# Token sums at another byte, attention from h's first result, and three smaller moves in a decoder layer on one core

## The chip, the cores and the metric

The kernel runs on 1 core of one Trainium2 chip. The metric is the device time of one execution in microseconds (us). All inputs and the output are float32.

## The reference

One decoder layer on 512 tokens of width 2048: a combined input projection, differential attention with 8 heads beside a gated short convolution, an output projection, and a SwiGLU feed-forward network of width 5632, each half between two RMS norms.

```python
hn = rms_norm(x, norm_mix_pre[l])
proj = hn @ w_in[l]                       # 2048 -> 6 x 1024
q, k, v, gate_b, gate_c, hc = jnp.split(proj, split_at, axis=-1)
...
a = diff_attention(q, k, v, lam, rel_bias)
a = rms_norm(a, subln_gain[l], SUBLN_EPS) * (1.0 - lambda_init)
a = a.reshape(b, s, A)
c = gate_b * short_conv(gate_c * hc, conv_w[l])
c = rms_norm(c, conv_norm_gain[l])
mix = jnp.concatenate([a, c], axis=-1) @ w_out[l]
x = x + rms_norm(mix, norm_mix_post[l])
hn = rms_norm(x, norm_ffn_pre[l])
f = (jax.nn.silu(hn @ w_gate[l]) * (hn @ w_up[l])) @ w_down[l]
x = x + rms_norm(f, norm_ffn_post[l])
```

In `diff_attention` a head has two softmaxes over 64 channels each, w = softmax(q1 k1 + bias) - lam * softmax(q2 k2 + bias), causal, and the output is w v.

## The kernel before

**Products.** Every float32 product of the large matrices is three matmuls (L133 to L135): both operands are split into a high part (a cast, on ACT, L99) and a low part (the rest, a subtraction on DVE, L100), and high x high, high x low and low x high are summed in PSUM. Weights come from HBM by DMA into raw tiles, are split into the four places of the ring `ring_all`, and feed PE from there. The normed tokens stay in one tile, `acts`, as `act_hi` and `act_lo`.

**Stages.** The start norms x and computes the first half of v (bank after bank pv, one for each of four blocks of 128 tokens, t). Then come jobs in a list; `run_jobs` runs them in order and gives a step of the side work (`side`) between their steps:

- the second half of v, with the token sums `t_sums` as side work;
- `project`: q, k and the first 256 columns each of h and c, as 10 quartets of 256 columns (8 for q and k, then h and c), each by 7 products instead of 8 (Strassen). A product is 24 matmuls of 128x256. Four of the seven (5, 7, 6, 4) read sums of token blocks, kept in `t_all` at the offset that `t_part` gives; three (1, 2, 3) read `acts`. In quartets 1 and 4 (`CLOSE_QK`) the products 1, 2, 5, 7 stand in this order, in the others 1, 5, 7, 2, and the instruction order lets four matmuls of one product through ahead of the one before;
- `open_attn` closes the pool `wino` (t_all, odd_raw, the r tiles) and opens `attn` in its place;
- column jobs (`job_cols`) of 256 columns: h1, b0, c1, b1, h2, c2, b2, h3, c3, b3, each with two halves of K and two banks pc, so 24 matmuls of 128x512 for each half and bank (a step), with the gated convolution in `done_h`, `done_c`, `done_b`. Attention is side work beside them: `heads` starts, in each step, the scores of one query block (pss, L658, then bias and exponential on DVE and ACT into e), the transposed weights of the block before (ptw, L688) and the values of the one before that (pa, L701); `head_out` (pta) ends a head. With 8 heads of 4 blocks that is some 37 steps. `load_attn`, a job after h1, issues the loads of q and k of head 0, of v and of the convolution's y, and puts `heads` on the side list. b0 and b1 are `finer`: they also give a side step in the middle of each 24 matmuls;
- output projection, residual, norms;
- `ffn`: gate and up in quartets by 7 products (banks pa, pb, pd), with token sums in tiles x and weight sums made by `combine(q, s)`: the sum s = 1 of the next quartet after product 3 of this one, in place in the order on DVE; only for q == HEAD it is held behind the low part of the split of product 3 (`issue_after`). `store_h` writes the hidden values out;
- down projection, and `down_last`, which adds the last products, norms a block of 128 tokens and stores it: per block t four pieces of 512 columns, each one DVE operation f * r + x (L1514) and a store, from SP's queue for even and from ACT's for odd pieces.

**What sets the order.** Each engine runs its own queue in order. PE's order is that of the program's steps, and PE waits for whichever operand is last. A new tile in a pool that opens where another was closed waits for the whole use of the old one.

**Places.** The operands' start in a partition, modulo 512 bytes, is fixed by the pools: `act_hi` and `act_lo` in `project` 480, the ring there 32; in `ffn` the tokens 416, the token sums in x 32, the ring 480. `t_all` starts at byte 20512 before, and its first sum 16 elements on, at 96 of 512.

Of the kernel before, what the change touches and what calls it, by code (L numbers as in the profile page):

```python
# [11 lines left out]
F32 = mybir.dt.float32  # L12
F32R = mybir.dt.float32r
AF = mybir.ActivationFunctionType
ALU = mybir.AluOpType
# [3 lines left out]
P = 128  # L19
D = 2048  # L20
S = 512
NT = S // P
KC = D // P
A = 1024
NH = 8
# [30 lines left out]
def trunk(ctx: ExitStack, tc: tile.TileContext, a, out):  # L56
    nc = tc.nc
    w_in, w_out, w_gate, w_up, w_down = (a[n][0] for n in ("w_in", "w_out", "w_gate", "w_up", "w_down"))
    x = a["x"][0]
    out = out[0]  # L60
# [102 lines left out]
    side = []  # L163
    done_ = object()

    def add_job(specs, go, ahead=1):
        jobs.append((specs, go, ahead))
# [142 lines left out]

    wino = ExitStack()
    wn = wino.enter_context(tc.tile_pool(name="wino", bufs=1))
    t_all = wn.tile([P, 8 * D + 16], F32R, name="t_all")
    odd_raw = [wn.tile([P, D], F32, name=f"odd{i}") for i in range(2)]


# [4 lines left out]
    for i in range(2):  # L321
        nc.vector.tensor_tensor_reduce(
            out=lamv[:, 2 * i, :], in0=lamv[:, 2 * i, :], in1=lamv[:, 2 * i + 1, :], scale=1.0, scalar=0.0,
            op0=ALU.mult, op1=ALU.add, accum_out=lamd[:, i : i + 1],
# [19 lines left out]

    def evacuate(cg, t, bank):

        if t % 2 == 0:
            tmp["v"] = wn.tile([P, 2, 512], F32, tag="r", bufs=2, name=f"r_v{cg}_{t}")
        nc.scalar.copy(tmp["v"][:, t % 2, :], bank)
        if t % 2:  # L350
            nc.sync.dma_start(vd[:, t - 1 : t + 1, cg * 512 : (cg + 1) * 512], tmp["v"])

    tmp = {}
    for t in range(NT):
        evacuate(0, t, vb[t])

# [3 lines left out]
    def open_attn(_):  # L360
        nonlocal ap_, aT, cT, v_sb, sqacc, klos
        wino.close()
        ap_ = at.enter_context(tc.tile_pool(name="attn", bufs=1))
        v_sb = ap_.tile([P, NT, A], F32, name="v_sb")
        aT = ap_.tile([P, NH, S], F32, name="aT")
        cT = ap_.tile([P, 8, S], F32, name="cT")
        sqacc = ap_.tile([P, S], F32, name="sqacc")

        klos = [ap_.tile([P, 2, S], F32R, name=f"klo{i}") for i in range(2)]
        for t in klos:  # L370
            nc.gpsimd.memset(t.bitcast(F32), 0.0)
        return
        yield

    def load_attn(_):
        load_qk(0)
        nc.sync.dma_start(v_sb, vd)
        nc.sync.dma_start(cT[:, 0:2, :], yd)
        side.append(heads(range(NH)))
        return  # L380
        yield

# [19 lines left out]
    def col_spec(w, c0, half, name):  # L402
        return w[half * 1024 : (half + 1) * 1024, c0 : c0 + 256], 8, 256, f"{name}_{half}"

    def job_cols(w, c0, name, done, finer=False):

        banks = []

        def part(half):
            def go(ch):  # L410
                (hi, lo), = ch
                for j in range(2):
                    if half == 0:
                        banks.append(mm_bank(f"pc_{name}_{j}"))
                    for k in range(8):
                        kc = 8 * half + k
                        cs = slice(j * P, (j + 1) * P)
                        mm3(banks[j], hi[:, k, cs], lo[:, k, cs], act_hi[:, :, kc, :], act_lo[:, :, kc, :], kc == 0, kc == KC - 1)
                        if finer and k == 3:
                            yield  # L420
                    if half == 1:
                        done(j, banks[j])
                    yield

            return go

        for half in range(2):
            add_job([col_spec(w, c0, half, name)], part(half))
# [15 lines left out]
    raws_qk, operands_qk = {}, {}  # L444

    def t_part(i, part):
        return t_all[:, 16 + (2 * T_PLACE[i] + part) * D :][:, :D].rearrange("p (t k n) -> p t k n", t=2, n=P)

    def t_sums():

# [272 lines left out]
    held = {}  # L723

    def done_h(j, b):
        t = ap_.tile([P, S + 2], F32, tag="hs", bufs=2, name=f"hs_{j}")
        nc.gpsimd.memset(t[:, 0:2], 0.0)
        nc.scalar.copy(t[:, 2:], b)
        held[j] = t
# [35 lines left out]
    for p in range(1, 4):  # L765
        job_cols(w_in, 5 * A + p * 256, f"h{p}", done_h)
        if p == 1:
            add_job([], load_attn)
            job_cols(w_in, 3 * A, "b0", done_b(0), finer=True)
        job_cols(w_in, 4 * A + p * 256, f"c{p}", done_c(p))  # L770
        job_cols(w_in, 3 * A + p * 256, f"b{p}", done_b(p), finer=p == 1)

    def as_tokens(t):
        return t.rearrange("p (t n) -> p t n", n=P)
# [624 lines left out]
    def ffn(_):  # L1399
        ready, ng = 7, len(order)  # L1400
        for n in (5, 6):
            prepare(n)
        for n, (q, i) in enumerate(order):
            product(n)
            yield
            gather(n)
            if n == 4:
                load_quartet(1)
            if q + 1 < HEAD and i in (6, 3):
                combine(q + 1, {6: 1, 3: 3}[i] if q else {3: 1, 6: 3}[i])  # L1410
            elif q < last_q and i == 3:

                with tc.issue_after(made[q, 3][1]) if q == HEAD else ExitStack():
                    combine(q + 1, 1)
            while ready < n + (5 if ready < ng and order[ready] in STAGED else 4):
                prepare(ready)
                ready += 1
            if i == 7 and q > 0:
                finish(q - 1)
            if i == 6 and q > 0:  # L1420
                store_h(q - 1)
            if q == last_q:

                for j, t in {1: ((1, 0),), 2: ((1, 1), (2, 0), (2, 1)), 5: ((5, 0),), 3: ((5, 1), (3, 0), (3, 1))}.get(
                    i, ((i, 0), (i, 1))
                ):
                    load_slot(j, 0, (t,))
        finish(last_q)
        store_h(last_q)
        load_block(1, 0)  # L1430
        for n, (g, cb, i, hf) in enumerate(steps):
            in_turn(steps_down, n, n + 2 if i == 3 and hf == 0 and 4 * g + cb in CLOSE_D else None, 7)
            yield
            gather_down(n)
            while ready < min(ng + n + 4, ng + len(steps)):
                prepare(ready)
                ready += 1
            if cb == 3 and hf == 1:
                load_slot(i, g + 1)
            if g == 2 and cb == 3:  # L1440
                tail_loads(i, hf)
# [37 lines left out]
    def down_last(_):  # L1479
        for t in range(NT):  # L1480
            xt = place(f"x{4 + t % 2}")
            nc.sync.dma_start(xt, x1d[t])

            pieces = [(cg, 0, 512) for cg in range(4)]
            if t == NT - 1:
                pieces[3:] = [(3, 0, 256), (3, 256, 256)]
            n = len(pieces)
            ssf = small.tile([P, n], F32, tag=f"ss{n}", name=f"ssf_{t}")
            for at_, (cg, c0, w_) in enumerate(pieces):
                cs, ws = slice(cg * 512 + c0, cg * 512 + c0 + w_), slice(c0, c0 + w_)  # L1490
                m = late["f"][:, t, cs]
                b = (mm_bank, aux_bank)[t % 2](f"pd_l_{cg}_{t}_{c0}")[:, :w_]
                for k in range(4):
                    ks = 4 * (k % 2) + t
                    mm3(
                        b, act_hi[:, k // 2, ks, :], act_lo[:, k // 2, ks, :], ch[cg][0][:, k, ws], ch[cg][1][:, k, ws],
                        k == 0, k == 3,
                    )
                nc.vector.tensor_add(m, m, b)
                nc.scalar.activation(b, m, AF.Square, accum_out=ssf[:, at_ : at_ + 1])  # L1500
                if at_ == n - 1:
                    ss = small.tile([P, 1], F32, tag="ss1", name=f"ssl_{t}")
                    v = small.tile([P, 1], F32, tag="v1", name=f"v_fin{t}")
                    nc.vector.reduce_sum(ss, ssf, axis=mybir.AxisListType.X)
                    mean = nc.vector.tensor_scalar(out=v, in0=ss, scalar1=1.0 / D, scalar2=EPS, op0=ALU.mult, op1=ALU.add)
                    r = small.tile([P, 1], F32, tag="r1", name=f"r_fin{t}")
                    nc.gpsimd.tensor_tensor(out=r, in0=v, in1=mhalf[:, :1], op=ALU.pow)
                with tc.issue_after(mean.ins) if (t, at_) == (NT - 1, n - 1) else ExitStack():
                    nc.vector.tensor_mul(m, m, late["gfin"][:, cs])
                if c0 + w_ == 512:  # L1510
                    yield
            for c in range(4):
                cs = slice(c * 512, (c + 1) * 512)
                nc.vector.scalar_tensor_tensor(  # L1514
                    out=xt[:, cs], in0=late["f"][:, t, cs], scalar=r, in1=xt[:, cs], op0=ALU.mult, op1=ALU.add
                )
                (nc.scalar if c % 2 else nc.sync).dma_start(out[t * P : (t + 1) * P, cs], xt[:, cs])

    add_job([], ffn, ahead=0)
# [29 lines left out]
```

## Time and profile before

| what | us |
|---|---|
| median of 3 runs | 2069.55 (2068.45 to 2071.57) |
| the profiled execution | 2067.07 |
| its span, first to last instruction | 2065.3 |
| start with the first half of v; second half of v | 0 to 113.2 |
| `project` | 113.2 to 311.4 |
| column jobs with attention | 311.4 to 594 |
| output projection, residual, start of `ffn` | 594 to 850 |
| gate and up | 850 to 1630 |
| down and the end | 1630 to 2065.3 |

A profile row of a group gives line, engine, operation, tiles (out<-in), shape and count, then the busy time in all, the mean of one in ns, and the idle time of the engine before, with what ended it. A matmul's duration is longer than the step from one start to the next, since matmuls are pipelined; the step is read from the start times in the timeline, or from the time of a stretch over its count. A row of the waits names the engine and operation that waited, and for what. A row of the windows gives the stretch, its length, PE's busy time with the number of matmuls, the granted clock, the DMA's busy share and GB/s.

### The profile page before, as it was taken

The page shows a single profiled execution, that of the slowest core. Times are in us where ns is not written, and L with a number is a line of the kernel's source. Part 1 is how long each engine was busy: PE and PEld are TensorE (multiplying, and loading weights), DVE is VectorE, ACT ScalarE, POOL GpSimd, SP SyncE. Part 2 cuts the span into 40 slices and gives each one's busy share as a digit, 9 for nine tenths or more (in the row PEclk, how much of TensorE's full clock was granted, in tenths as well). Part 3 has the DMA queues.
Part 4 walks back from the last instruction along what each step waited for, and adds up shares of the span by engine and source line. Part 5 has one row for each costly group of instructions (what it writes and reads, how often), then busy time and mean ns, then how long its engine had stood idle before and what let it go on. Part 6 is the DMA issues. An engine that isn't in the chain of part 4 may idle for free.

```text
span 2065.3 us, 36338 instructions
## 1 busy us (share of the span) xinstructions
PE 2044.6 (99%) x15356; PEld 1939.9 (94%) x15356; DVE 1626.4 (79%) x2058; ACT 969.3 (47%) x1361; POOL 27.4 (1%) x49
## 2 busy tenths in 40 slices
PE   9999999999999999999999999999999999999998
PEld 7899998888888889999999999999999999999996
DVE  5777767887465468989888988889889777888887
ACT  4444445664334354544544544544554444434442
POOL 0000001000000000000000000000000000000000
PEclk9999999999999999999999999999999999999999
DMA  7444326322239857654554653554654955748354
GB/s 244 131 160 143 124 93 211 100 92 87 82 107 363 299 208 288 194 159 131 181 159 125 187 159 125 187 159 124 188 159 132 331 179 198 266 126 301 112 190 163
DMA packets 301907, 359.64 MB, mean 174 GB/s; under 512 B 11912, under 2 KB 261768, under 8 KB 295856
## 3 DMA queue, kind: packets, MB, share of 16 engines
q1 hardware_dynamic: 300144, 351.53, 51.3%
q10 hardware_dynamic: 1600, 5.79, 0.9%
q8 instruction: 120, 1.97, 0.4%
q14 instruction: 43, 0.35, 0.1%
HBM read 289.64 MB, written 70.28 MB: 174 GB/s over the span
## 4 chain that ended last, share of the span: by engine, by line
PE 90%; DVE 4%; DMA 2%; issue 2%; ACT 1%; POOL 0%; SPq 0%; DVEq 0%; POOLq 0%; ACTq 0%
PE pb L134 7%; PE pb L133 7%; PE pb L135 7%; PE pd L135 6%; PE pd L134 6%; PE pd L133 6%; PE pa L133 5%; PE pa L134 5%; PE pa L135 5%; PE po L133 3%; PE po L134 3%; PE po L135 3%; PE pqk_b L133 2%; PE pqk_b L135 2%; PE pqk_b L134 2%
## 5 line engine op out<-in xcount | busy, mean ns | idle before, releaser
L99 ACT CAST ring_all<-raw_q 128x1024 fp32r<-128x1024 f32 x124 | 129.8, 1050 | 189.0 <-PE pb L134 72.3
L134 PE MATMUL pb<-x,ring_all 128*128 128x256 f32 x696 | 194.8, 280 | 0.0
L134 PE MATMUL pb<-acts,ring_all 128*128 128x256 f32 x704 | 194.5, 276 | 0.0
L133 PE MATMUL pb<-acts,ring_all 128*128 128x256 f32 x704 | 194.5, 276 | 0.0
L135 PE MATMUL pb<-acts,ring_all 128*128 128x256 f32 x704 | 194.4, 276 | 0.0
L133 PE MATMUL pb<-x,ring_all 128*128 128x256 f32 x696 | 194.2, 279 | 0.0
L135 PE MATMUL pb<-x,ring_all 128*128 128x256 f32 x696 | 194.2, 279 | 0.0
L133 PE MATMUL pa<-acts,ring_all 128*128 128x256 f32 x680 | 188.6, 277 | 0.0
L134 PE MATMUL pa<-acts,ring_all 128*128 128x256 f32 x680 | 188.1, 277 | 0.0
L135 PE MATMUL pa<-acts,ring_all 128*128 128x256 f32 x680 | 187.9, 276 | 0.0
L135 PE MATMUL pd<-ring_all,acts 128*128 128x256 f32 x640 | 176.8, 276 | 0.3 <-DMA acts<-hx 0.3
L133 PE MATMUL pd<-ring_all,acts 128*128 128x256 f32 x640 | 176.8, 276 | 0.0
L134 PE MATMUL pd<-ring_all,acts 128*128 128x256 f32 x640 | 176.7, 276 | 0.0
L99 ACT CAST ring_all<-pre 128x1024 fp32r<-128x1024 f32 (+1 forms) x106 | 105.1, 996 | 141.0 <-PE pb L134 73.7
L100 DVE TENSOR_TENSOR ring_all<-raw_q,ring_all 128x1024 fp32r<-128x1024 f32 x124 | 151.5, 1222 | 22.4 <-ACT ring_all L99 22.1
L100 DVE TENSOR_TENSOR ring_all<-pre,ring_all 128x1024 fp32r<-128x1024 f32 (+1 forms) x106 | 122.1, 1155 | 46.3 <-ACT ring_all L99 45.6
L99 ACT CAST ring_all<-post 128x1024 fp32r<-128x1024 f32 (+1 forms) x106 | 105.2, 994 | 95.7 <-PE pd L135 38.7
L100 DVE TENSOR_TENSOR ring_all<-post,ring_all 128x1024 fp32r<-128x1024 f32 (+1 forms) x106 | 121.9, 1150 | 15.1 <-ACT ring_all L99 15.1
L134 PE MATMUL pd<-ring_all,x 128*128 128x256 f32 x480 | 132.6, 276 | 0.3 <-DVE ring_all L100 0.3
L135 PE MATMUL pd<-ring_all,x 128*128 128x256 f32 x480 | 132.5, 276 | 0.0
L133 PE MATMUL pd<-ring_all,x 128*128 128x256 f32 x480 | 132.5, 276 | 0.0
L133 PEld LDWEIGHTS pb<-acts,ring_all 128*128 128x128 f32 x704 | 132.2, 188 | 0.0
(358 smaller groups left out, 6598.8 us busy)
## 6 DMA issues: line engine op xcount, KB each, us to landing
raw_q<-in_w_gate SPq DMA_DIRECT2D x42, 1024.0 KB, 5.4
post<-in_w_up SPq DMA_DIRECT2D x22, 1024.0 KB, 5.2
pre<-in_w_up SPq DMA_DIRECT2D x22, 1024.0 KB, 5.3
hx<-spare SPq DMA_DIRECT2D x20, 896.0 KB, 8.2
hx<-m SPq DMA_DIRECT2D x20, 896.0 KB, 8.9
raw_o<-in_w_out SPq DMA_DIRECT2D x16, 1024.0 KB, 8.0
raw_b<-in_w_down SPq DMA_DIRECT2D x16, 896.0 KB, 5.9
acts<-hx SPq DMA_DIRECT2D x32, 448.0 KB, 9.0
```

Source lines behind the costliest of these rows:

```text
L99: first = nc.scalar.copy(hi, src)
L100: second = nc.vector.tensor_tensor(out=lo, in0=src, in1=hi.bitcast(F32), op=ALU.subtract)
L133: yield nc.tensor.matmul(o, lhsT=lhi, rhs=rhi, start=start, stop=False, **kw).ins
L134: yield nc.tensor.matmul(o, lhsT=lhi, rhs=rlo, start=False, stop=False, **kw).ins
L135: yield nc.tensor.matmul(o, lhsT=llo, rhs=rhi, start=False, stop=stop, **kw).ins
```

## The change

Five things, in one diff:

1. The token sums start 112 elements into `t_all` instead of 16. With part 2 `t_all` begins at byte 28704, and the first sum at 480 of 512, the same as act_hi and act_lo in `project`.
2. The first tile for v's copies, r_v0_0, is allocated ahead of `t_all`, in the place where `t_all` began.
3. The loads of `load_attn` move into `open_attn`, ahead of h1, and `heads` is put on the side list by the first `done_h`, in the last steps of h1. `finer` is gone: every column job gives a side step after each 24 matmuls only.
4. The sum s = 1 for the quartet after HEAD - 1 is held behind the split of product 3 too.
5. In the last token block the piece c = 2 is scaled on ACT and added on GpSimd (POOL), where DVE did both in one operation.

```diff
+    tmp = {"v": wn.tile([P, 2, 512], F32, tag="r", bufs=2, name="r_v0_0")}
-    t_all = wn.tile([P, 8 * D + 16], F32R, name="t_all")
+    t_all = wn.tile([P, 8 * D + 112], F32R, name="t_all")
...
     def evacuate(cg, t, bank):
-        if t % 2 == 0:
+        if t % 2 == 0 and (cg, t) != (0, 0):
             tmp["v"] = wn.tile([P, 2, 512], F32, tag="r", bufs=2, name=f"r_v{cg}_{t}")
...
-    tmp = {}
...
             nc.gpsimd.memset(t.bitcast(F32), 0.0)
-        return
-        yield
-
-    def load_attn(_):
         load_qk(0)
         nc.sync.dma_start(v_sb, vd)
         nc.sync.dma_start(cT[:, 0:2, :], yd)
-        side.append(heads(range(NH)))
...
-    def job_cols(w, c0, name, done, finer=False):
+    def job_cols(w, c0, name, done):
...
-                        if finer and k == 3:
-                            yield
...
-        return t_all[:, 16 + (2 * T_PLACE[i] + part) * D :][:, :D].rearrange("p (t k n) -> p t k n", t=2, n=P)
+        return t_all[:, 112 + (2 * T_PLACE[i] + part) * D :][:, :D].rearrange("p (t k n) -> p t k n", t=2, n=P)
...
     def done_h(j, b):
+        if "begun" not in held:
+            held["begun"] = True
+            side.append(heads(range(NH)))
...
         if p == 1:
-            add_job([], load_attn)
-            job_cols(w_in, 3 * A, "b0", done_b(0), finer=True)
+            job_cols(w_in, 3 * A, "b0", done_b(0))
         job_cols(w_in, 4 * A + p * 256, f"c{p}", done_c(p))
-        job_cols(w_in, 3 * A + p * 256, f"b{p}", done_b(p), finer=p == 1)
+        job_cols(w_in, 3 * A + p * 256, f"b{p}", done_b(p))
...
-                with tc.issue_after(made[q, 3][1]) if q == HEAD else ExitStack():
+                with tc.issue_after(made[q, 3][1]) if q in (HEAD - 1, HEAD) else ExitStack():
                     combine(q + 1, 1)
...
-                nc.vector.scalar_tensor_tensor(
-                    out=xt[:, cs], in0=late["f"][:, t, cs], scalar=r, in1=xt[:, cs], op0=ALU.mult, op1=ALU.add
-                )
+                m = late["f"][:, t, cs]
+                if (t, c) == (NT - 1, 2):
+                    nc.scalar.activation(m, m, AF.Copy, scale=r)
+                    nc.gpsimd.tensor_tensor(out=xt[:, cs], in0=m, in1=xt[:, cs], op=ALU.add)
+                else:
+                    nc.vector.scalar_tensor_tensor(out=xt[:, cs], in0=m, scalar=r, in1=xt[:, cs], op0=ALU.mult, op1=ALU.add)
```

How the change moves instructions, at three places. First PE's queue where attention begins; pss are the first scores of head 0, q and k its operands, pc_b0_0 and pc_b0_1 the two banks of b0, pc_h1_1 the second of h1. Before:

```order
L135 MATMUL pc_b0_0_3024<-acts_72,ring_all_73 128x512
L658 MATMUL pss_0_0_0_3070<-k_0_3038,q_0_3037 128x128
L659 MATMUL pss_0_0_0_3070<-klo0_2905,q_0_3037 128x128
L658 MATMUL pss_0_0_1_3071<-k_0_3038,q_0_3037 128x128
L659 MATMUL pss_0_0_1_3071<-klo0_2905,q_0_3037 128x128
L133 MATMUL pc_b0_1_3089<-acts_72,ring_all_73 128x512
```

In this place of the changed kernel's queue, at the end of h1:

```order
L135 MATMUL pc_h1_1_2937<-acts_72,ring_all_73 128x512
L651 MATMUL pss_0_0_0_3041<-k_0_2994,q_0_2993 128x128
L652 MATMUL pss_0_0_0_3041<-klo0_2905,q_0_2993 128x128
L651 MATMUL pss_0_0_1_3042<-k_0_2994,q_0_2993 128x128
L652 MATMUL pss_0_0_1_3042<-klo0_2905,q_0_2993 128x128
L133 MATMUL pc_b0_0_3064<-acts_72,ring_all_73 128x512
```

The first scores moved ahead by the 24 matmuls of b0's first bank; the scores after them (pss_0_1) stand 24 matmuls on instead of 12, and the first transpose (ptw_0_0) 8 matmuls after those, in b0's second bank.

Second, DVE's queue in `ffn` where the first sum of quartet 4 is made (m1 from the two raw tiles raw_q4); post and pre are the weights of the quartet at work, and ring_all<-post and ring_all<-pre the low parts of their splits. Before:

```order
L100 TENSOR_TENSOR ring_all_73<-post_55_7158,ring_all_73 128x1024
L1068 TENSOR_TENSOR m1_52_6979<-raw_q4_0_7305,raw_q4_1_7306 128x1024
L1235 TENSOR_TENSOR m3_57_7309<-m3_57_7309,spare_58_7315 128x1792
L1072 TENSOR_TENSOR post_55_7158<-pre_56_7159,post_55_7158 128x8x128
L1197 TENSOR_TENSOR m0_53_7010<-pb_2_7248,m1_52_6979 128x512
L1074 TENSOR_TENSOR pre_56_7159<-pre_56_7159,post_55_7158 128x8x128
L100 TENSOR_TENSOR ring_all_73<-post_55_7158,ring_all_73 128x1024
L1070 TENSOR_TENSOR raw_q4_0_7305<-raw_q4_0_7305 128x8x128
L100 TENSOR_TENSOR ring_all_73<-pre_56_7159,ring_all_73 128x1024 x2
```

The same piece of the changed kernel:

```order
L100 TENSOR_TENSOR ring_all_73<-post_55_7158,ring_all_73 128x1024
L1068 TENSOR_TENSOR post_55_7158<-pre_56_7159,post_55_7158 128x8x128
L1231 TENSOR_TENSOR m3_57_7309<-m3_57_7309,spare_58_7315 128x1792
L100 TENSOR_TENSOR ring_all_73<-post_55_7158,ring_all_73 128x1024
L1193 TENSOR_TENSOR m0_53_7010<-pb_2_7248,m1_52_6979 128x512
L1070 TENSOR_TENSOR pre_56_7159<-pre_56_7159,post_55_7158 128x8x128
L100 TENSOR_TENSOR ring_all_73<-pre_56_7159,ring_all_73 128x1024 x2
L1064 TENSOR_TENSOR m1_52_6979<-raw_q4_0_7305,raw_q4_1_7306 128x1024
L1179 TENSOR_TENSOR m2_54_7011<-m2_54_7011 128x256
```

The sum (L1068 before, L1064 after) moved from the second row to behind the three splits, and raw_q4's next difference (L1070 before) further on still.

Third, ACT's queue at the end, where f holds the last block and pd_l its last banks. Before:

```order
L1500 ACTIVATE pd_l_3_0_20202,ssf_20185<-f 128x512
L1500 ACTIVATE pd_l_3_0_20218,ssf_20185<-f 128x512
L1500 ACTIVATE pd_l_3_0_20234,ssf_20185<-f 128x256
L1500 ACTIVATE pd_l_3_256_20250,ssf_20185<-f 128x256
L1517 DMA out<-x_192_20183 128x512 x2
```

And in the changed kernel:

```order
L1496 ACTIVATE pd_l_3_0_20218,ssf_20185<-f 128x512
L1496 ACTIVATE pd_l_3_0_20234,ssf_20185<-f 128x256
L1496 ACTIVATE pd_l_3_256_20250,ssf_20185<-f 128x256
L1513 ACTIVATE f<-f,r_fin_20269 128x512
L1517 DMA out<-x_192_20183 128x512 x2
```

ACT's scaling (L1513) is new ahead of its two stores; DVE's last row (f * r + x) counts three pieces instead of four, and POOL has one new row behind the last r_fin, the addition into x_192.

## The prediction

> **What bounds the kernel now.** I read the page's first part, then the busy time by stage, then the waits of PE, and only then single instructions.
>
> ```profile
> PE 2044.6 (99%) x15356; PEld 1939.9 (94%) x15356; DVE 1626.4 (79%) x2058; ACT 969.3 (47%) x1361; POOL 27.4 (1%) x49
> ```
>
> PE is busy for 2044.6 of 2065.3 us, so time can come off in two ways only: PE waits less, or its matmuls follow each other more closely. The PE windows of four stages show both (busy us, number of matmuls, granted clock):
>
> ```profile
> 113.20:311.40 198.20, 198.20 (x1681) 1.00 0.37 123
> 333.20:424.00 90.80, 87.61 (x454) 1.00 0.38 125
> 424.00:594.00 170.00, 169.81 (x843) 1.00 0.26 84
> 850.00:1630.00 780.00, 779.97 (x6754) 1.00 0.52 161
> ```
>
> At full clock and without a wait, `project` (113.2 to 311.4) takes 198.20/1681 = 117.9 ns from one matmul to the next, while gate/up (850 to 1630) takes 780.0/6754 = 115.5 ns, with the same tile of 128x256. Column jobs b0, c1 and b1 (333.2 to 424) leave PE idle for 90.80 - 87.61 = 3.2 us; the jobs after them leave 0.2 us. The waits of PE that the change touches, over the whole span (total, times, longest):
>
> ```profile
> PE pa L701 <- DVE wlo L100: 1.4, 2, 0.9
> ...
> PE pd L135 <- DVE ring_all L100: 1.2, 1, 1.2
> PE ptw L688 <- DVE e L677: 0.9, 2, 0.7
> PE pa L701 <- ACT aT L721: 0.9, 1, 0.9
> PE pv L133 <- ACT r_v L349: 0.7, 1, 0.7
> ```
>
> **Part 1, the token sums' place.** First the mean duration by form, in `project` (two rows), then in gate/up (three rows; each form has three such rows, L133 to L135):
>
> ```profile
> L133 PE MATMUL pqk_b<-t_all,ring_all 128*128 128x256 f32 x240 | 67.2, 280 | 0.0
> ...
> L133 PE MATMUL pqk_a<-acts,ring_all 128*128 128x256 f32 x160 | 45.0, 281 | 0.0
> ```
>
> ```profile
> L134 PE MATMUL pb<-x,ring_all 128*128 128x256 f32 x647 | 181.2, 280 | 0.0
> ...
> L133 PE MATMUL pb<-acts,ring_all 128*128 128x256 f32 x644 | 177.8, 276 | 0.0
> ...
> L133 PE MATMUL pa<-x,ring_all 128*128 128x256 f32 x320 | 89.3, 279 | 0.0
> ```
>
> The same tile `acts` as moving operand costs 276 ns in gate/up and 281 in `project`; sums cost 279 to 280 in both. So there are two paces. In gate/up the slow one belongs to 1942 (pb) and 960 (pa) matmuls on sums in x. At 117.9 ns those take 342.1 us, which leaves (780.0 - 342.1)/3852 = 113.7 ns for the others: **4.2 ns** between the paces. In gate/up the operands lie at bytes 416 (acts) and 32 (x) of 512; in `project` at 480 (acts) and 96 (t_all), after the change at 480 both. That an operand's own place isn't all of it is shown by `acts` in `project`: slow, except at one spot, the "close" order of quartet 1 (as in quartet 4), where four matmuls on t_all are cut in ahead of a product on acts:
>
> ```profile
> 136.19 0.28 PE L133 MATMUL pqk_b<-t_all,ring_all 128*128 128x256 f32 x1
> 136.46 0.39 PE L133 MATMUL pqk_a<-acts,ring_all 128*128 128x256 f32 x1
> ...
> 136.80 0.28 PE L135 MATMUL pqk_a<-acts,ring_all 128*128 128x256 f32 x1
> ...
> 139.18 0.28 PE L135 MATMUL pqk_a<-acts,ring_all 128*128 128x256 f32 x1
> 139.29 0.28 PE L134 MATMUL pqk_b<-t_all,ring_all 128*128 128x256 f32 x1
> ```
>
> From 136.80 to 139.18 lie 21 steps: 113.3 ns each, the quick pace, on an operand that was slow until then. The next product reads t_all again, and the slow pace is back for good. So a pace is a state: it holds while the moving operand's byte stays, and it may turn when that byte changes or after such a short stop. With one byte for acts and t_all nothing changes it back. I take it that `project` starts slow as now (its first product reads acts and is slow), turns quick at the close at 136.5 us, and stays so. From 139.2 to 311.4 there are 172.2/0.1179 = 1460 matmuls, less the 24 that are quick now at the second close: 1436 x 4.2 ns = **-6.0 us**. The bounds are 0 (the pace never turns) and 1656 x 4.2 = -7.0 (quick from the first product).
>
> The Trainium skill, "TensorE: Matmul & The Clock Gate", section "Wait — 56ns, not 53.3ns?", gives a warm start-to-start of N/2.4 GHz plus about 2.5 ns, whatever the operand's address; as an estimate 109.2 ns for N = 256. Neither pace above is that, and the page knows no second one; by it this part would be worth nothing, which is the first rival below.
>
> **Part 2, v's copies.** r_v0_0 now takes the place at which t_all began.
>
> ```profile
> 69.55 0.50 PE L133 MATMUL pv<-ring_all,acts 128*128 128x512 f32 x1 [0.72 <-ACT r_v L349]
> ```
>
> The first copy empties the bank which the next v product needs. In both programs it waits for the same last matmul of the first half, since new tiles of this pool wait for the whole pool before. I cost it at **0** (bounds -0.7, the whole wait, and 0, since nothing is added).
>
> **Part 3, attention.** Same instructions, other places: heads begin four matmuls after h1's last one instead of 24 into b0, and b0 and b1 lose their half steps (12 matmuls between attention steps), so that 24 matmuls stand between a score and what follows, as in the stage from 424 on, which idles 0.2 us. That would remove the 3.2 us. New is the first chain. From the timelines of PE, DVE, POOL and ACT before:
>
> ```profile
> 333.19 0.39 PE L133 MATMUL pc_b<-acts,ring_all 128*128 128x512 f32 x1
> ...
> 338.63 0.23 PE L658 MATMUL pss<-k,q 128*128 128x128 f32 x1
> ...
> 339.03 0.44 PE L133 MATMUL pc_b<-acts,ring_all 128*128 128x512 f32 x1
> ...
> 341.84 0.28 PE L658 MATMUL pss<-k,q 128*128 128x256 f32 x1
> ```
>
> ```profile
> 330.11 0.69 DVE L618 TENSOR_TENSOR klo<-aT,k 64x512 fp32r<-64x512 f32 x1 [1.06 <-ACT k L616]
> ...
> 335.14 2.29 DVE L100 TENSOR_TENSOR ring_all<-raw_b,ring_all 128x2048 fp32r<-128x2048 f32 x1 [2.05 <-ACT ring_all L99]
> ...
> 342.71 0.35 DVE L677 SCALAR_TENSOR_TENSOR e<-e,rs 128x128 f32<-128x128 f32 x1
> ```
>
> ```profile
> 335.45 2.13 POOL L645 TENSOR_SCALAR_AFFINE_SELECT bt<-bt 128x128 f32<-128x128 f32 x1 [11.42 <-DMA bt<-d]
> ```
>
> ```profile
> 338.69 0.62 ACT L617 CAST k<-aT 64x512 fp32r<-64x512 f32 x1
> 341.08 0.40 ACT L670 ACTIVATE e<-e,mx 128x128 f32<-128x128 f32 x1 [1.77 <-DVE mx L668]
> ...
> 341.78 0.19 ACT L670 ACTIVATION_READ_ACCUMULATOR e<-e,mx 128x1 f32 x1
> ```
>
> q and k of head 0 are ready at 330.8, so the scores at 333.2 don't wait. The bias bt is masked at 337.6 and DVE's split of b0's second chunk ends at 337.4; neither moves. ACT's queue keeps the casts for head 1 ahead of the exponentials, to 339.3; with 0.9 us for these (341.08 to 341.97), one klo subtraction of 0.7 that stands ahead on DVE, and 1.8 us of small steps (my estimate; those of the same chain took 343.06 - 341.97 = 1.1 us before, with two fewer steps between them), e is ready at 342.7, where it was at 343.06. PE reaches its transpose after the scores (338.63 to 339.03, 0.4), 24 matmuls (333.19 to 338.63, 5.4), the second scores (0.5) and 8 matmuls (two thirds of the 2.8 us that 12 took from 339.03), so at 341.4: a **wait of 1.3 us** in place of the 0.7 there now. Queued behind it on PE are the column jobs themselves, so it counts in full. Sum -3.2 + 1.3 = **-1.9 us**; bounds -4.0 (no new wait, and the slow refill after each old one gone too) and +1.5 (the wait of 1.3 comes twice more). SP's queue keeps the weights of b0 ahead of the attention's loads, and yd's store is issued long before; the last head's values and output now stand in b3, whose end PE reaches with aT's splits where they were.
>
> **Part 4, quartet 4's sum of gate/up.** DVE and PE before:
>
> ```profile
> 838.47 1.22 DVE L1068 TENSOR_TENSOR m<-raw_q,raw_q 128x1024 f32<-128x1024 f32 x1 [1.28 <-DMA raw_q<-in_w_gate]
> ...
> 844.42 1.22 DVE L100 TENSOR_TENSOR ring_all<-post,ring_all 128x1024 fp32r<-128x1024 f32 x1
> ```
>
> ```profile
> 844.21 0.28 PE L134 MATMUL pd<-x,ring_all 128*128 128x256 f32 x1
> 845.69 0.39 PE L135 MATMUL pd<-x,ring_all 128*128 128x256 f32 x1 [1.21 <-DVE ring_all L100]
> ```
>
> The sum waits 1.28 us for a load and holds DVE's queue, with the ring split for which PE then waits 1.21 us behind it. Now the sum stands behind three ring splits; the split of post comes 1.28 + 1.22 us earlier at least, ahead of PE's need at 844.4. Nothing that is moved ahead depends on the load, and DVE's work is the same. **-1.2 us** (bounds -1.5, with the refill of PE, and 0, if the next split, of raw_q, becomes late by as much).
>
> **Part 5, the last piece.** The timeline of the end, ACT's nearest group, and the DMA's load from 2057 to 2066 (slices of 0.225 us):
>
> ```profile
> 2058.44 0.59 POOL L1507 TENSOR_TENSOR r_fin<-v_fin,mhalf 128x1 f32<-128x1 f32 x1 [9.65 <-DVE v_fin L1505]
> 2059.07 2.74 DVE L1514 SCALAR_TENSOR_TENSOR x<-f,r_fin,x 128x512 f32<-128x512 f32 x4 [0.44 <-POOL r_fin L1507]
> ```
>
> ```profile
> L1500 ACT ACTIVATE pd_l<-f 128x512 f32<-128x512 f32 x15 | 9.0, 597 | 30.9 <-DVE f L1499 30.9
> ```
>
> ```profile
> GB/s 0 0 0 0 0 0 0 0 0 0 0 0 0 0 0 0 209 400 355 392 382 355 392 355 319 392 373 337 291 109 0 0 0 0 0 0 0 0 0 0
> ```
>
> DVE does three pieces rather than four and ends 0.66 us earlier. But the four stores of 256 KB already flow without a gap at 320 to 400 GB/s for 3.0 us; at a steady 390 they'd take 2.7, so the end gains 0.3 at most. ACT scales the third piece in about 0.6 us (597 ns for a square of the same size), to 2059.7. POOL's add of 128x512 with two inputs isn't in the trace; it lies between POOL's 0.59 (128x1) and the 2.13 above (128x128, beside DVE's two-input split at 335.14). With 1.2, its store is ready at 2060.9, unneeded before; with 2.13 it is last at 2061.8, as now. I take **0** (bounds -0.3 and +0.5).
>
> The Trainium skill speaks against this part: "SBUF — State Buffer", section "Who interferes with whom", has a DVE operation with two SBUF inputs contend with a GpSimd instruction that reads SBUF, whoever comes second being blocked. With a further 0.75 us of DVE ahead of POOL the sum would be some 0.4 us worse; the 2.13 us above agrees with that rule.
>
> **The sum:** -6.0 + 0 - 1.9 - 1.2 + 0 = -9.1 us. The profiled execution took 2067.07 us (span 2065.3), 2.5 below the median of the runs, 2069.55; that gives 2058.0 from the one and 2060.4 from the other, and I say **2059**.
>
> **The rivals.** (a) *The pace stays slow*: the state is set at the first product of `project`, which the change leaves as it is, and one byte for all means that nothing turns it. For: in gate/up the pace changes with the byte alone. Against: the quick product above came with a stop that stays. Then -3.1 us: 2065. (b) *It turns at the second close only*, at 196 us: 115 us less, 955 x 4.2 = -4.0 in place of -6.0: 2061. (c) *Attention falls behind*, and the kernel is slower: ACT and DVE prepare head 1 and split weights in the same 8 us as the first chain, and PE reaches each transpose ahead of DVE. DVE is the engine: if its work per attention step exceeds PE's 24 matmuls and attention, about 7 us, the 1.3 us recurs in all 12 steps of b0, c1 and b1: +15.6 us, and with no gain from the pace, 2059 + 6.0 + 15.6 - 1.3 = 2079; with it 2073. Against: from 424 on the same rate of steps leaves 0.2 us idle. (d) *v's copies move after all*: -0.7 more.
>
> **The numbers.** My forecast has 0.60 with (d) inside, (a) 0.25, (b) 0.08, (c) 0.06, something else 0.01. What a measurement of this kernel can tell from no change is about 0.2%, 4.1 us: below 2065.4 is faster. (a) sits on that edge, the larger part above it: 0.08 faster, 0.17 same. With 0.05 of the forecast lost to poorer attention and pace together, faster has 0.71, same 0.23, slower 0.06. The range takes the low bounds of pace, attention and part 4 together at 2054 and (a) with part 3 lost at 2067.5.
>
> **What would show it.** Right: in `project` the groups on t_all and acts at 276 to 277 ns, 1681 matmuls in about 192 us; the waits for wlo and aT gone between 311 and 424, one wait of ptw for e of about 1.3 us left; no wait of pd for ring_all near 845; the r_v wait still 0.7; the last stores' flow the same. Wrong: t_all at 280 ns to the end of `project`, waits of PE in each step up to 424, or another pace in gate/up, where this change moves nothing but a stop at 845: if quick and slow changed places there, (3852 - 2902) x 4.2 = 4.0 us would be lost.

## The result, and the profile after

The changed kernel takes 2060.26 us (median of 21 runs, 2055.88 to 2074.54), the kernel before on the same chips 2070.22: a ratio of 0.9946 with a 95% interval of 0.9923 to 0.997, so 6 to 16 us less. The profiled execution has a span of 2059.0 us where before it was 2065.3. The range and the side of the prediction hold; its 2059 lies 1.3 us off. In six of the 21 executions of each kernel (and in five of the 13 of the kernel before with which the run with the tokens at 32 is compared) the time lies 12 to 19 us above the others, at the same granted clock where that is recorded; no profile here caught such an execution, so it stays unexplained, and the medians of the others are 2058.7 and 2069.5 us.

First the busy time and the waits of PE over the span, which answer to the first lines and the waits shown for before:

```profile
PE 2038.0 (99%) x15356; PEld 1936.4 (94%) x15356; DVE 1626.9 (79%) x2057; ACT 968.5 (47%) x1362; POOL 28.6 (1%) x50
```

```profile
PE ptw L681 <- DVE e L670: 2.4, 2, 1.8
...
PE pd L133 <- DMA acts<-hx: 1.4, 1, 1.4
...
PE pd L133 <- ACT m L1178: 1.1, 1, 1.1
PE pv L133 <- ACT r_v L350: 0.7, 1, 0.7
PE pd L135 <- DMA acts<-hx: 0.6, 1, 0.6
```

The waits for wlo and aT and the 1.2 us for ring_all are gone. A longer one for e stands in place of the first two, the wait for v's copy is the same 0.7, and two are new, at 793 us for a copy of a bank and at 1623 us for loads.

PE's busy time fell by 6.6 us, though it runs the same 15356 matmuls. The windows of `project`, ahead of its first close and behind it, and the rows by form from the second part, show where:

```profile
113.83:136.40 22.57, 22.57 (x193) 1.00 0.36 123
139.90:305.65 165.75, 165.74 (x1462) 1.00 0.39 127
```

```profile
L135 PE MATMUL pqk_b<-t_all,ring_all 128*128 128x256 f32 x215 | 59.3, 276 | 0.0
...
L134 PE MATMUL pqk_a<-acts,ring_all 128*128 128x256 f32 x129 | 35.6, 276 | 0.0
```

Up to the close 22.57/193 = 116.9 ns from start to start (118 in the timeline; the count takes in one or two matmuls across the edges), behind it 165.75/1462 = 113.4 ns, on t_all and on acts alike. Both forms now have 276 ns where they had 280 and 281.

Where the time went, by the starts of each stage's first matmul in the profiled executions (us; "end" begins with the last products pd_l). The kernel before and the changed one were each profiled a second time:

| kernel | start | `project` | column jobs with attention | output projection | gate/up | down | end | span |
|---|---|---|---|---|---|---|---|---|
| before | 113.2 | 198.2 | 276.7 | 182.6 | 859.6 | 382.3 | 52.7 | 2065.3 |
| before, again | 113.4 | 196.7 | 277.1 | 182.6 | 860.7 | 383.8 | 52.7 | 2067.1 |
| changed | 113.8 | 191.8 | 274.0 | 182.6 | 859.7 | 384.0 | 53.1 | 2059.0 |
| changed, again | 113.8 | 191.8 | 273.1 | 182.6 | 861.5 | 387.4 | 53.1 | 2063.3 |
| sums at 96 | 113.3 | 196.7 | 273.2 | 182.6 | 858.0 | 384.0 | 53.1 | 2061.0 |
| only the sums | 113.6 | 194.1 | 276.8 | 182.6 | 859.8 | 383.5 | 52.7 | 2063.0 |
| close in quartet 4 only | 113.7 | 193.8 | 273.4 | 182.6 | 857.6 | 384.8 | 53.1 | 2059.0 |
| no close | 113.4 | 197.9 | 273.8 | 182.6 | 859.0 | 383.6 | 53.1 | 2063.4 |
| sum of quartet 4 in place | 113.2 | 191.8 | 273.3 | 182.6 | 858.9 | 383.5 | 53.1 | 2056.4 |
| end all on DVE | 113.4 | 191.8 | 273.1 | 182.6 | 859.3 | 385.6 | 52.7 | 2058.5 |
| only attention | 113.3 | 196.7 | 273.9 | 182.6 | 860.8 | 385.2 | 52.7 | 2065.3 |

`project` gives 4.9 to 6.4 us and the column jobs 2.7 to 4.0. The end costs 0.4. Gate/up and down differ by up to 3.5 us between two executions of one kernel.

### The profile page after: what moved, and what is told of

The parts are those of the page before. It is cut to its first block, busy times and chain, and to the rows that moved or that the text cites. A ratio compares the mean times of both kernels' runs of the same rounds, so it can differ in the third digit from the quotient of the medians.

```text
span 2059.0 us, 36347 instructions
## 1 busy us (share of the span) xinstructions
PE 2038.0 (99%) x15356; PEld 1936.4 (94%) x15356; DVE 1626.9 (79%) x2057; ACT 968.5 (47%) x1362; POOL 28.6 (1%) x50
## 4 chain that ended last, share of the span: by engine, by line
PE 92%; DVE 3%; DMA 2%; issue 1%; ACT 1%; POOL 0%; SPq 0%; DVEq 0%; POOLq 0%; ACTq 0%
PE pb L134 7%; PE pb L133 7%; PE pb L135 7%; PE pd L134 6%; PE pd L133 6%; PE pd L135 6%; PE pa L133 5%; PE pa L134 5%; PE pa L135 5%; PE po L135 3%; PE po L133 3%; PE po L134 3%; PE pqk_b L134 2%; PE pqk_b L135 2%; PE pqk_b L133 2%
```

## The experiments

**The sums back at byte 96, and the sums alone.** The first in the changed kernel, the second in the kernel before (with `t_all` 96 elements longer):

```diff
-        return t_all[:, 112 + (2 * T_PLACE[i] + part) * D :][:, :D]...
+        return t_all[:, 16 + (2 * T_PLACE[i] + part) * D :][:, :D]...
```

> The changed kernel with the token sums 16 instead of 112 elements into t_all, so at byte 96 of 512 again; everything else as changed. Theory (the pace of 128x256 matmuls is a state that holds while the moving operand's byte stays): `project` slow but for the two close products, 198.2 us instead of 191.8, the span 6.3 us longer than the changed kernel's. Rival (t_all's new start at 28704 or r_v0_0's place did it): `project` stays at 192 us and the span within 1 us of the changed kernel's.

> The kernel before with the sums alone moved, 112 elements in, byte 480 at the old start 20512. Theory: `project` 191.8 us instead of 198.2, the quick pace from the close at 136 us on; attention, gate/up and the end as before; the span 6 us shorter, 2059. Rival: no change of `project`, the span 2065.

Measured: a ratio to before of 0.998 (0.997 to 0.9989) with the sums back, of 0.9978 (0.9969 to 0.9988) with the sums alone; multiplied, 0.9958, within the interval of the whole change. `project` took 196.7 and 194.1 us. So the sums' byte is worth 4.5 us by itself and about 7 as the rest of the whole change (0.9946/0.998; the interval of the whole change leaves 2 to 12), wherever t_all starts, and the rival falls. But neither figure is the expected one, and both for the same reason: the state may turn at the second close as well as at the first. With the sums alone, the windows ahead of and behind the second close read:

```profile
113.61:195.80 82.19, 82.19 (x697) 1.00 0.39 130
199.30:307.66 108.36, 108.36 (x958) 1.00 0.37 121
```

117.9 and 113.1 ns: slow through the first close, quick only from the second on. Whether that was chance or came of t_all's old start, this one profile can't tell. With the sums at 96, `project` isn't slow throughout behind the second close:

```profile
L134 PE MATMUL pqk_b<-t_all,ring_all 128*128 128x256 f32 x128 | 35.8, 280 | 0.0
...
L134 PE MATMUL pqk_a<-acts,ring_all 128*128 128x256 f32 x80 | 22.1, 276 | 0.0
```

There acts is quick and t_all slow, product by product, as acts and x are in gate/up. The second profile of the unchanged kernel before does the same (196.7 us). So the kernel before too has two courses in `project`, and the change is worth 6.4 us against the one and 4.9 against the other.

**The closes.** What turns the pace, tried by taking closes out of the changed kernel:

```diff
-    LAST_QK, CLOSE_QK = len(COLS_QK) - 1, (1, 4)
+    LAST_QK, CLOSE_QK = len(COLS_QK) - 1, (4,)
```

and the same with `()`.

> The changed kernel with the close order in quartet 4 only (CLOSE_QK = (4,)). Theory (with one byte for all, only the stop of a close turns the pace): slow from 114 to 195 us, quick behind, so `project` takes 198.2 - 24 products of 0.11 us of the changed kernel's gain, about 194.5 us, +2.5 us to the changed kernel. Rival (the pace turns by itself after some time, about 23 us into `project`): quick from 137 us, 191.8 us.

> The changed kernel without close orders in `project` (CLOSE_QK = ()). Theory: slow to the end, 198 us or a little more if a bank is waited for. Rival (time or address alone): quick from some point on, under 195 us. If a wait for a bank comes in where the close stood, that stop turns the pace there, and the theory expects the turn at that stop.

The windows of the first around its only close, and the one of `project` without any:

```profile
113.72:195.60 81.88, 81.88 (x697) 1.00 0.39 131
199.20:307.50 108.30, 108.30 (x958) 1.00 0.37 121
```

```profile
113.40:311.26 197.86, 197.86 (x1681) 1.00 0.37 123
```

Slow for 82 us and quick behind the stop; slow to the end without a stop (117.7 ns). That was the sharpest test, with one profile each: with one byte for all operands nothing but the stop turned the pace, and neither time nor address alone makes it quick. A stop doesn't always turn it, as the first close with the sums alone shows. `project` took 193.8 us in the first, 0.7 less than the rough sum expected.

**More closes.** In quartets 0 to 4, with the end all on DVE:

> The changed kernel with the last four pieces all on DVE, and with the close order in quartets 0 to 4 of `project` instead of 1 and 4, to give the pace more chances to turn and an earlier one. Theory: each close costs 0.26 us; if the one of quartet 0 turns the pace, quick from 117 us on, `project` about 191.8 - 0.8 + 0.8 = 191.8 us, and 194 or more in fewer executions than now; end stage 52.65 instead of 53.05; the median 0.4 us or more below the changed kernel's, too little to be told from it. Rival (a close turns the pace either way with like chance, as at the closes of gate/up in the run with tokens at 32): more closes leave `project` as a mixture, 193 to 197 us.

The ratio to before is 0.9956 (0.9942 to 0.997, median 2059.18), not to be told from the changed kernel's. Quartet 0's close turned the pace at 117.7 us, and none of the four closes behind it turned it back:

```profile
117.70:306.10 188.40, 188.37 (x1654) 1.00 0.38 126
```

That is 113.9 ns with the stops. But `project` took 192.9 us: at quartet 0 PE waits 0.8 us for a split that isn't ready so early (just ahead of the turn, so that wait may have turned it too), and each stop has its price. Nothing won.

**Another byte near by.** Sums 96 elements into t_all, at byte 416, acts at 480:

> The changed kernel with the token sums 96 elements into t_all, so at byte 416 of 512, 64 bytes below acts at 480. Theory (any change of the moving operand's byte within 512 may turn the pace): products on t_all and on acts keep different paces, or all slow, as in the kernel with sums at 96 (128 bytes off): 196 to 198 us. Rival (what counts is a coarser place, 128 bytes or more): as with the same byte, quick for both from a close on, 192 to 194 us.

```profile
L135 PE MATMUL pqk_b<-t_all,ring_all 128*128 128x256 f32 x240 | 67.7, 282 | 0.0
...
L134 PE MATMUL pqk_a<-acts,ring_all 128*128 128x256 f32 x160 | 44.5, 278 | 0.0
```

t_all is slower than in any other run (119 ns from start to start in the timeline), acts a mixture of both paces, `project` 198.2 us. A difference of 64 bytes is enough; the rival falls.

**The same step in gate/up.** The tokens of `ffn` at byte 32, where the sums in x are:

```diff
-        for o in (16, 144 + NT * KC * P, 0, 128 + NT * KC * P)
+        for o in (16, 144 + NT * KC * P, 32, 32 + NT * KC * P)
```

> The changed kernel with the same step taken in gate/up: the tokens of `ffn` start 32 elements into acts (their low parts 32 + 8192), so at byte 32 of 512 like the token sums in x, instead of 416. Theory (a pace is a state that holds while the moving byte stays, a stop may turn it): one pace for all 128x256 matmuls of gate/up over long stretches, slow until a close or another stop turns it (the closes of quartets 5, 7, 12 and 24) and quick behind it, where now only 3852 of 6754 are quick: up to 2902 x 4.4 ns = 12.8 us less than the changed kernel's 860 us in that stage, and 16 us more if it never turns. Rival (acts are quick because of byte 416, x slow because of byte 32): all slow, 16 us more, and no stop changes it.

The ratio is 1.0 (0.9971 to 1.0028) and gate/up takes 874.2 us, 14.5 more than in the changed kernel. Its stretches between closes:

```profile
779.00:867.00 88.00, 85.97 (x740) 1.00 0.68 225
867.80:905.70 37.90, 37.90 (x333) 1.00 0.44 135
906.30:1004.80 98.50, 98.50 (x836) 1.00 0.50 153
1005.50:1242.50 237.00, 237.00 (x2012) 1.00 0.50 154
1243.20:1635.70 392.50, 392.50 (x3332) 1.00 0.52 163
```

The close of quartet 5 turned everything quick (37.90/333 = 113.8 ns, on x at byte 32 too, which the rival excludes); the close of quartet 7 turned it slow again (117.8), and those of 12 and 24 left it so. With one byte the pace is one for all over long stretches, as in `project`, but a stop can turn it either way, and here it fell on the slow side for 90% of the stage.

The first row hides two more turns. From 799.7 to 837.7 us all matmuls were quick (113.3 ns by the start times), and there a step of 1.1 us, a wait for a bank not yet copied and no close, turned them slow. The quick pace had come at 799.7 us without a stop, where the weights, with x as moving operand throughout, changed from the tile w (119.6 ns) to the ring. So the weights' place may count too; no run moved it by itself. With two bytes about half of gate/up's matmuls are quick in each execution (3332 to 3900 of some 7390, counted from the start times, in all others).

**Quartet 4's sum back in place.**

```diff
-                with tc.issue_after(made[q, 3][1]) if q in (HEAD - 1, HEAD) else ExitStack():
+                with tc.issue_after(made[q, 3][1]) if q == HEAD else ExitStack():
```

> The changed kernel with quartet 4's sum back in its old place on DVE. Theory: the wait of pd for ring_all comes back (1.2 us, a step of about 1.4), less what PE is late there anyway. Rival (the load has landed by then, since PE's gain ahead doesn't move it): no wait, no difference.

The timeline of DVE, and PE's waits from 800 to 860 us:

```profile
828.05 1.23 DVE L1064 TENSOR_TENSOR m<-raw_q,raw_q 128x1024 f32<-128x1024 f32 x1 [1.05 <-DMA raw_q<-in_w_gate]
...
833.99 1.22 DVE L100 TENSOR_TENSOR ring_all<-post,ring_all 128x1024 fp32r<-128x1024 f32 x1
```

```profile
PE pd L135 <- DVE ring_all L100: 1.1, 1, 1.1
```

The wait is back, as expected, where the changed kernel has none; there the sum stands behind the splits:

```profile
832.64 1.22 DVE L100 TENSOR_TENSOR ring_all<-post,ring_all 128x1024 fp32r<-128x1024 f32 x1
...
838.81 1.22 DVE L1064 TENSOR_TENSOR m<-raw_q,raw_q 128x1024 f32<-128x1024 f32 x1
```

Yet gate/up took 858.9 us here and 859.7 in the changed kernel. What hides the gain is the spread of the stage. With 4.4 ns taken off for each slow matmul, the five profiles with the sum in its old place (two of before, the sums alone, attention alone, and this one) come to 843.4 to 844.7 us, mean 844.0, and the eight with the sum moved (all but that with tokens at 32) to 842.0 to 843.8, mean 842.9: 1.1 us, which a single pair of executions can't show. The two groups overlap, and four of the first five lack other parts of the change too, so the size is an estimate.

**The end all on DVE.** The changed kernel with `if False:` in place of the condition of the last piece.

> The changed kernel with the last four pieces all on DVE as before. Theory (POOL's add holds DVE's next piece, and the stores have a gap): from the first piece on DVE to the end of the span 6.2 us as in the kernel before instead of 6.6, so 0.4 us less. Rival (the stores bound the end either way): the same 6.6.

The timelines of DVE (all three pieces in one row, then the last of them in a narrower stretch) and of POOL, and the DMA's rate (2050 to 2060, slices of 0.25 us) in the changed kernel:

```profile
2052.36 3.08 DVE L1516 SCALAR_TENSOR_TENSOR x<-f,r_fin,x 128x512 f32<-128x512 f32 x3 [0.44 <-POOL r_fin L1503]
...
2053.70 1.75 DVE L1516 SCALAR_TENSOR_TENSOR x<-f,r_fin,x 128x512 f32<-128x512 f32 x1
```

```profile
2053.16 1.74 POOL L1514 TENSOR_TENSOR x<-f,x 128x512 f32<-128x512 f32 x1 [0.83 <-ACT f L1513]
```

```profile
GB/s 0 0 0 0 0 0 0 0 0 0 0 0 0 0 0 49 360 360 361 385 377 205 0 344 369 393 385 369 238 0 0 0 0 0 0 0 0 0 0 0
```

and DVE with all four pieces:

```profile
2052.30 2.74 DVE L1516 SCALAR_TENSOR_TENSOR x<-f,r_fin,x 128x512 f32<-128x512 f32 x4 [0.44 <-POOL r_fin L1503]
```

Three pieces beside POOL's add take DVE longer (3.08 us) than four alone (2.74), since the third lasts 1.75 us, where a piece of the four takes some 0.74: it ends 0.55 us behind POOL's add. The stores run dry for a slice in the middle, and the end stage is 53.1 instead of 52.7 us, in every kernel with the add against every one without it. The theory holds.

**Attention alone**, in the kernel before:

> The kernel before with part 3 alone (loads in open_attn, heads begun by h1's first result, no half steps). Theory: from h1's first matmul to the output projection's first 274.0 us as in the changed kernel instead of 276.7: the three waits for wlo and aT gone, one or two of ptw for e left. Rival (those 2.7 us came from the pace or from other conditions in the changed kernel): 276 or more. `project` stays slow, 198 us.

273.9 us, as expected, with waits of PE for e only:

```profile
PE ptw L683 <- DVE e L672: 2.3, 2, 1.7
```

The saving is the edit's own. The span, 2065.3, doesn't show it, since gate/up and down took 4.1 us more than in the first profile of before (1.5 more than in the second). `project` took 196.7 us, by the second course of the kernel before, not 198.

**Both kernels once more.**

> The kernel before, unchanged, profiled a second time. It tells how far stages differ from one execution to the next. Theory (the wait of pd for acts<-hx at the start of down, 0.3 us in the first profile of before and 0.9 to 2.4 in the others, is spread of the loads and no effect of the change): between 0.3 and 2.4 us here too, not tied to how early PE comes. Rival (PE comes earlier and the loads don't, so the change's gain is given back there): 0.3 again. `project` slow, 198 us; attention 276.7; end stage 52.7.

> The changed kernel, unchanged, profiled a second time. Theory: attention 273 to 274 us, end stage 53.05, wait of pd for ring_all near 845 gone; `project` 191.8 us if its first close turns the pace, 194 if only the second does, 198 if none does; gate/up and the start of down within 2 us of the first profile either way, by stops that turn the pace there and by the loads. Rival (the pace's turn is fixed by the program): 191.8 exactly.

They are in the table. `project` took exactly 191.8 us again. The wait of pd for loads at the start of down was 0.6 us in the kernel before and 2.6 in the changed one (2.0 + 0.6):

```profile
PE pd L133 <- DMA acts<-hx: 2.0, 1, 2.0
PE pd L135 <- DMA acts<-hx: 0.6, 1, 0.6
```

Over all fourteen profiles, down's first wait was 0.3 to 0.6 us in the three whose PE gets there at 1630 us or later (both of before, and the tokens at 32), and 1.3 to 2.6 in the eleven that come by 1627. That speaks for the rival, that some of the gain is given back there, though the second profile of before waits another 0.9 us for loads (of x) at 1652 us, so 1.5 in all. But the loads are issued as PE releases their places and came 8.4 us earlier with it (the first at 1605.3 instead of 1613.7), so I don't know what they wait for. It stays open; no run took that wait away.

What makes down 3.4 us longer in the second execution of the changed kernel than in the first is mostly the clock. Right behind that wait the granted clock was 0.50 for 6.8 us, and 30 matmuls ran where the next stretch of the same length has 62:

```profile
1626.70:1633.50 6.80, 6.19 (x30) 0.50 1.02 376
1633.60:1640.40 6.80, 6.80 (x62) 1.00 0.82 282
```

At 213 instead of 113 ns a step, those 30 cost 3.0 us. The same shows behind this wait with the sums at byte 416 (6.8 us) and, for 3.4 us, with the end all on DVE; these are the kernels whose down took 387.2 and 385.6 us. The other eleven profiles keep a clock of 1.00 there, also that with more closes, which waits as long (1.9 + 0.6 us), so the wait's length alone doesn't decide it.

## Why the prediction was right, by its own steps

- **Part 1**, -6.0 us: right in mechanism and spot, and near in size. `project` starts slow, turns at the close (136.5 us before, 137 now), stays quick through the second close: 198.2 - 191.8 = 6.4 against the first profile of before, 4.9 against the second. What the prediction took too firmly is that the close turns the pace. With one byte throughout, the first close turned it in each profile with closes as in the changed kernel at those sums, but not with the sums alone, and a close of gate/up turned it back. It was also not seen that the kernel before has a second, better course (196.7); against that the forecast was too high.
- **Part 2**, 0: right, the wait for r_v is 0.7 us in every profile.
- **Part 3**, -1.9 us: the sign was right, the size too small: -2.7 in the first pair of profiles and -4.0 in the second. The step that failed is the sum of waits alone. The new wait was mis-sized (0.9 to 1.8 us for 1.3, and a second of 0.6 not foreseen), so idle time fell only from 3.4 to 2.5. The rest came from PE's busy time, 273.3 to 271.5 us, as the windows show:

```profile
311.41:588.07 276.66, 273.28 (x1363) 1.00 0.34 113
```

```profile
305.65:579.64 273.99, 271.53 (x1362) 1.00 0.35 114
```

  By the start times the attention steps broke the column jobs' matmuls 50 times before and 36 times now. That breaks are what cost the 1.75 us is argued from this count, not shown by a run of its own.
- **Part 4**, -1.2 us: the wait went as forecast, and 1.1 us is the difference of the means above. The step it left out is that another wait can stand behind: in the second profile of the changed kernel, and likewise with more closes and with the tokens at 32, PE waited 0.8 to 0.9 us for a bank not yet copied, some 2 us later in the stage than the old wait (in the second profile at 838 us):

```profile
PE pb L133 <- ACT m L1178: 0.8, 1, 0.8
```

  None of the other eleven profiles has it. The 1.1 us at 793 in the first profile is no effect of this part: it comes some 45 us ahead of the moved sum (838.81), and at that place of the stage PE's longest step lies between 0.19 and 1.5 us over the fourteen profiles.
- **Part 5**, 0 (bounds -0.3 and +0.5): +0.4. The step that was too hopeful is POOL's 1.2 us with nothing held up: its add took 1.74, 0.6 of it beside DVE's second piece, and DVE's last piece took 1.75 for some 0.74. The rule of the Trainium skill that the prediction weighed there ("SBUF — State Buffer", "Who interferes with whom") agrees with these rows: DVE's last piece, with two SBUF inputs, ended only 0.55 us after POOL's add. The 0.4 us that the prediction worked out beside that rule, and didn't take, is what came.
- **The total.** By the table the first pair of profiles differs by -6.3 us and the second by -3.7, while the medians differ by 10.0. In the first pair `project`, the column jobs and the end give -6.4 - 2.7 + 0.4 = -8.7; the start, gate/up and down, for which only part 4's -1.2 was forecast, give +0.6, +0.1 and +1.7. That the sum of -9.1 met the medians to within 1.3 us is thus partly luck: parts that were too small (1 and 3) stand against what the end and down took back.
- **The rivals.** (a) fell, and would have come true without closes: 197.9 us. (b) came true in the kernel with the sums alone. (c) fell: DVE keeps up at even steps. (d) fell. The section "Wait — 56ns, not 53.3ns?" of "TensorE: Matmul & The Clock Gate" in the Trainium skill has one warm step, 109.2 ns for N = 256 as the prediction estimated from it. Here, with float32 operands, it is 113.3 or 117.9 ns for the same tile at full clock, and for this kernel the measurement decides.

## What to carry to other kernels

Where PE is the bound, divide a stage's time by its matmuls: two stages with one tile and different steps point to something that no list of waits shows. Give the operands that take turns as moving operand the same byte within 512, and then look at which pace they share, because it can be the slow one: it gained 4.9 to 6.4 us in `project` and lost 14.5 in gate/up. And see whether an engine that helps at the end holds up the one that it helps.

## What the runs showed of the hardware

At a granted clock of 1.00, 128x256 matmuls have two main paces, 113.3 and 117.9 ns from one start to the next; some 119 to 120 ns show too, on sums 64 bytes off the tokens and with weights from the tile w. The pace of a stretch goes with the moving operand's place and with what went before. In `project`, with one place and all weights from the ring, it stayed for up to 198 us, and only a stop in PE's stream (of some 0.15 us at a close) turned it. In gate/up with one place it stayed for up to 392 us, and stops turned it in either direction; once it turned without one, as the weights changed from w to the ring. With places 64 or 128 bytes apart the paces of the two operands take turns, or both are slow: in the changed kernel a stop at 875 us (362 ns from one start to the next) left gate/up slow on acts and x until the close at 907. Which way a stop turns it wasn't found out, and it makes executions of one program differ by some microseconds: but for the run with the tokens at 32, gate/up had between 3474 and 4040 slow matmuls, at 4.4 ns each 2.5 us.

The granted clock can fall to 0.50 behind a wait in the middle of the kernel: for 3.4 to 6.8 us at the start of down in three of fourteen profiles, behind waits of 2.2 to 2.6 us.
